# Copies of x's rows by tokens: pinned on ScalarE and placed later, with the evacuation of the first down columns

## The chip, the cores and the metric

The kernel runs on one core of one Trainium2 chip. The metric is the device time of one execution in microseconds. The page of the profile shows one profiled execution; its own time and the median of three runs stand below.

## The reference

Two layers of a decoder trunk on 256 tokens of width 1024, in float32, then a final norm:

```python
def rmsnorm(x, g):
    y = x32 * lax.rsqrt(jnp.mean(x32 * x32, axis=-1, keepdims=True) + EPS)
    return y.astype(x.dtype) * g

def swiglu(x, w_gate, w_up, w_down):
    return (jax.nn.silu(x @ w_gate) * (x @ w_up)) @ w_down
...
    for l in range(DEPTH):
        x = x + 0.5 * swiglu(rmsnorm(x, ffn1_norm[l]), ffn1_w_gate[l], ffn1_w_up[l], ffn1_w_down[l])
...
        x = x + odd_mixer(h, od_w_in[i], od_w_out[i], rel_bias)
        x = x + memory_cross_attention(rmsnorm(x, xa_norm[l]), mem_n, xa_w_q[l], xa_w_kv[l], xa_w_o[l])
        x = x + 0.5 * swiglu(rmsnorm(x, ffn2_norm[l]), ffn2_w_gate[l], ffn2_w_up[l], ffn2_w_down[l])
    return rmsnorm(x, final_norm)
```

The hidden width of each SwiGLU is 2816, that is 22 tiles of 128. The change lies in the last one (ffn2 of layer 1) and the final norm.

## The kernel before

**Products.** x is held by channels: 128 channels on the partitions, 8 tiles, 256 tokens along the row. A float32 product is made of three TensorE passes with fp32r operands: each operand is split into a high part and a low part, and high x high, high x low and low x high are added in PSUM. So each weight tile goes through two steps: ScalarE copies it to `whi` (line 143), VectorE makes `wlo = raw - whi` (line 144). The class `Stream` runs this: SyncE loads chunks of 16 weight tiles (1 MB, line 117) into four `raw` buffers, and blocks of 8 tiles are split into five pairs of `whi` and `wlo`. A block's split can start when TensorE is done with the block five before; a raw buffer is loaded again when VectorE has read it.

**The last SwiGLU.** Its hidden rows are computed with tokens on the partitions, in groups of four tiles (`rows_of`, lines 575 to 577). Each group is turned back to hidden-by-token form by `turned_back`: VectorE transposes 32 x 32 squares (line 545), GpSimd's queue writes them to a DRAM tile `turn` and reads them back in four pieces (lines 547 and 549), and ScalarE and VectorE split the result into `h` (lines 557 and 558). The last such group has two tiles, 20 and 21; its target buffer is named `v`, so its read is `v<-turn` and its split is `h<-v`.

**The last down product** (`down_tok`) has tokens on the partitions, so that its result is already in the output's order. It multiplies `h` by the down weights (lines 791 to 793). First come columns 0 to 511 for both halves of the tokens (two PSUM tiles named `acc`), over all 22 hidden tiles, two at a time. Then come columns 512 to 1023, in three regions: tokens 0 to 127 whole (a PSUM tile named `sc`), tokens 128 to 255 in two halves of 256 columns (`acc`). The first 14 hidden tiles run for all three regions together, the last 8, whose splits stay in four buffers, run region by region.

**The residual by tokens.** For the final sum x is needed with tokens on the partitions. `to_tokens` writes x to a DRAM tile `tok`; `from_tokens` reads it into a tile named `bias` in four pieces on GpSimd's queue (line 839); `natural` copies it into `y`, a tile in the slot named `k2` (shown as `k`), in 16 ScalarE copies of 128 x 128 (line 847). `evac_tok` then adds half the down product (line 804), sums the squares (line 807), multiplies by the final norm's factors (GpSimd, line 810, or VectorE, line 814), and for the last columns scales by the norm and stores (lines 817 to 821).

**What sets the order.** `Order` keeps a model clock in nanoseconds. `pe.after(delay, fn, cost)` puts a task on a heap at the model time plus the delay; the fillers (matmul parts) move the clock by their cost. A task's place in the program comes from this. Behind it a scheduler may move instructions on an engine, except those passed through `tc.keep_in_program_order`, which stay in the written order. The splits of `h` in `turned_back` are pinned in this way; the copies at line 847 are not. Every engine runs its instructions in order, so an instruction that waits for a semaphore holds all behind it.

Of the kernel before, what the change touches and what calls it, by code (L numbers as in the profile page):

```python
# [17 lines left out]
AF = mybir.ActivationFunctionType  # L18
# [5 lines left out]
P = 128  # L24
# [216 lines left out]
def paired(t):  # L241

    return t.rearrange("p (b a) -> p a b", b=2)
# [22 lines left out]
def build(nc, tc, ctx, a):  # L266
# [18 lines left out]
    def w2():  # L285
        return act.tile([P, 512], F32, name="w2", bufs=6)
# [28 lines left out]
    pe = Order()  # L315
# [192 lines left out]
    def to_tokens(tok, k):  # L508


        t = act.tile([P, 2 * S], F32, name="q2", bufs=2)
        tc.keep_in_program_order(nc.vector.transpose(t.rearrange("q (a g j) -> q g a j", a=4, g=4),
                                                     x[:, k:k + 2].rearrange("p k (u a i) -> p (k u) a i", u=2, a=4)))
        tc.keep_in_program_order(nc.sync.dma_start(tok[k // 2], t))
# [19 lines left out]
    def ffn(which, layer, n, nxt, first=False, last=False):  # L534
# [206 lines left out]
        def have(ks):  # L741
            return lambda: math.inf if any(h[k] is None for k in ks) else 0.0
# [26 lines left out]
        def down_tok():  # L769

            late = 2 * (ws.BUFS - 1)
            pss, got, mean = {}, {}, [EPS, EPS]

            def part(fs, *regions):

                c = regions[0][1] // 512

                def go():  # L780
                    for f in fs:
                        if (f, c) not in got:
                            got[f, c] = ws.take(f"{which}_w_down", layer, f * P, c * 512, 4)
                        for reg in regions:
                            u, c0, c1 = reg
                            if f == 0:
                                pss[reg] = (sc_tile if c == 1 and c1 - c0 == 512 else acc_tile)()[:, :c1 - c0]
                            ps = pss[reg]
                            wh, wl = (paired(w)[:, (c0 - c * 512) // 2:(c1 - c * 512) // 2] for w in got[f, c])
                            hh, hl = (h[f].v[:, u, m] for m in range(2))  # L790
                            nc.tensor.matmul(ps, hh, wh, start=f == 0, stop=False)  # L791
                            nc.tensor.matmul(ps, hh, wl, start=False, stop=False)  # L792
                            nc.tensor.matmul(ps, hl, wh, start=False, stop=f == FT - 1)  # L793
                    if fs[-1] == FT - 1:
                        for u, c0, c1 in regions:
                            pe.after(0 if c else 6000, lambda u=u, at=slice(c0, c1), ps=pss[u, c0, c1]: evac_tok(u, at, ps), 0)

                return have(fs), go, sum(len(fs) * (c1 - c0) * 654 // 512 for _, c0, c1 in regions)

            def evac_tok(u, at, ps):  # L800
                xtok = back["y"]
                y = xtok[:, u, at]
                g = gfin[at.start // 512][:, at.start % 512:at.start % 512 + at.stop - at.start]
                nc.vector.scalar_tensor_tensor(y, ps, 0.5, y, op0=ALU.mult, op1=ALU.add)  # L804
                ms = act.tile([P, 1], F32, name="mean", bufs=4)
                junk = w2()[:, :at.stop - at.start]
                nc.vector.tensor_tensor_reduce(junk, y, y, 1.0 / D, mean[u], ALU.mult, ALU.add, ms)  # L807
                mean[u] = ms
                if at.stop < D:
                    nc.gpsimd.tensor_tensor(y, y, g, op=ALU.mult)  # L810
                    return
                r = act.tile([P, 1], F32, name="rcol", bufs=2)
                nc.gpsimd.tensor_tensor(r, ms, mhalf[:, 0:1], op=ALU.pow)
                nc.vector.tensor_tensor(y, y, g, op=ALU.mult)
                out = a["out"][u * P:(u + 1) * P]
                cuts = (0, 384, 704, D)
                nc.scalar.activation(xtok[:, u, :cuts[1]], xtok[:, u, :cuts[1]], AF.Copy, scale=r)
                nc.scalar.dma_start(out[:, :cuts[1]], xtok[:, u, :cuts[1]])
                for i, j in zip(cuts[1:], cuts[2:]):
                    nc.vector.tensor_scalar(xtok[:, u, i:j], xtok[:, u, i:j], r, None, op0=ALU.mult)  # L820
                    nc.sync.dma_start(out[:, i:j], xtok[:, u, i:j])

            end = range(FT - late, FT)
            right = ((0, 512, D), (1, 512, 768), (1, 768, D))
            return [part(range(i, i + 2), (0, 0, 512), (1, 0, 512)) for i in range(0, FT, 2)] + [
                part(range(FT - late), *right)] + [part(end, reg) for reg in right]
# [5 lines left out]
        if last:  # L832
            gfin = []
            tok, back = dram.tile([KT // 2, P, 2 * S], F32, name="tok"), {}

            def from_tokens():
                t = act.tile([P, 2 * D], F32, name="bias", bufs=1)
                for b in range(4):
                    tc.keep_in_program_order(nc.gpsimd.dma_start(
                        t[32 * b:32 * b + 32].rearrange("i (g z) -> i g z", g=16),  # L840
                        tok.rearrange("k (p i) (a z) -> a i (k p) z", p=4, a=4)[b]))
                v = t.rearrange("q (k p m u j) -> q u k m p j", k=4, p=4, m=2, u=2)

                def natural(k):
                    y = back["y"] = back.get("y") or act.tile([P, 2, D], F32, name="k2", bufs=1)
                    for u in range(2):
                        nc.scalar.activation(y[:, u, k * P:(k + 1) * P].rearrange("q (p j) -> q p j", p=4),  # L847
                                             v[:, u, k // 2, k % 2], AF.Copy)

                for k in range(KT):  # L850
                    pe.after(15000+700*k, lambda k=k: natural(k), 0)

            def last_factors():
                gfin.extend(act.tile([P, 512], F32, name="p2", bufs=4) for _ in range(2))
                src = a["final_norm"]
                for i, g in enumerate(gfin):
                    nc.sync.dma_start(g, bass.AP(tensor=src.tensor, offset=src.offset + i * 512, ap=[[0, P], [1, 512]]))

            pe.after(90000, last_factors, 0)
            for k in range(0, KT, 2):  # L860
                pe.after(16000 + 9000 * (k // 2), lambda k=k: to_tokens(tok, k), 0)
            pe.after(114500, from_tokens, 0)
        at = AT.get((which, layer))
        groups = [f0 for f0 in range(0, FT, 4) if at is None or f0 != SEVEN]
# [602 lines left out]
```

## Time and profile before

| | |
|---|---|
| three runs | 967.06, 958.13, 960.61 us (median 960.61) |
| the profiled execution | 960.96 us, span 958.9 us |
| TensorE busy | 947.4 us (99%), 5796 matmuls |
| VectorE, ScalarE, GpSimd busy | 726.1 (76%), 596.6 (62%), 119.2 us (12%) |
| HBM read and written | 220.81 MB and 16.80 MB, 248 GB/s over the span |
| last matmul | starts at 951.45 us |

A row of a timeline has the start, the duration, the engine, the line of the kernel, the operation, the tiles (out<-in without buffer numbers) and the count; in brackets stands how long the engine was idle before it, and what released it. Times count from the span's start. TensorE's rows are matmuls (PE) and weight loads (PEld); since matmuls are pipelined, their rate is read from the distance between starts and not from the duration. A row of the windows has, for a stretch, the busy time of PE, PEld, VectorE (DVE), ScalarE (ACT) and GpSimd (POOL), then the granted TensorE clock as a share of full speed, the share of the DMA engines and GB/s.

### The profile page before, as it was taken

Reading aid. Unit: us, or ns where it says so; the run is one execution under the profiler, and the core shown is the slowest. Engines: PE = TensorE matmul, PEld = TensorE weight load, DVE = VectorE, ACT = ScalarE, POOL = GpSimd, SP = SyncE. Lnnn points to the kernel's source line nnn. Section 1 sums busy time; section 2 is a strip of 40 time slices with the busy share of each in tenths; the row PEclk is TensorE's granted clock in tenths of the full one; section 3 lists DMA queues with packets and bytes.
Section 4 is the critical chain, followed back from the end, with each engine's and each line's share of the span. In section 5 each row is a group of like instructions: output and inputs, shape, how many; then the busy total and the mean of one; then the engine's idle time right before and its main releaser. Section 6 shows DMA issues by size and latency. Waiting matters only on the chain. (4 is left out here: it accounts for less than half of the span.)

```text
span 958.9 us, 15176 instructions
## 1 busy us (share of the span) xinstructions
PE 947.4 (99%) x5796; PEld 868.9 (91%) x5796; DVE 726.1 (76%) x1153; ACT 596.6 (62%) x984; POOL 119.2 (12%) x207
## 2 busy tenths in 40 slices
PE   9999999999999999999999999999999999999987
PEld 8888899999999888889988888999999998888876
DVE  7667667788878886976778697677777789688563
ACT  7555555697658866555576565556775787565451
POOL 0412210001000111121001112100000010202311
PEclk9999999999999999999999999999999999999999
DMA  9999975555536899889759978855534479999841
GB/s 375 314 349 327 327 230 211 180 188 198 183 133 247 233 262 335 254 303 335 246 176 268 334 235 300 288 204 194 218 133 176 150 246 304 274 321 316 260 148 44
DMA packets 39368, 235.44 MB, mean 246 GB/s; under 512 B 5624, under 2 KB 6648, under 8 KB 14720
## 3 DMA queue, kind: packets, MB, share of 16 engines
q1 hardware_dynamic: 26928, 182.43, 52.2%
q0 software_dynamic: 11792, 51.42, 20.7%
q8 instruction: 45, 0.74, 0.3%
q10 hardware_dynamic: 576, 0.64, 0.2%
q14 instruction: 27, 0.22, 0.1%
HBM read 220.81 MB, written 16.80 MB: 248 GB/s over the span
## 5 line engine op out<-in xcount | busy, mean ns | idle before, releaser
L144 DVE TENSOR_TENSOR wlo<-raw,whi 128x1024 fp32r<-128x1024 f32 (+2 forms) x363 | 409.2, 1139 | 145.7 <-ACT whi L143 143.1
L143 ACT ACTIVATE whi<-raw 128x1024 fp32r<-128x1024 f32 (+2 forms) x363 | 353.3, 985 | 235.7 <-PE acc L577 81.0
L576 PE MATMUL acc<-wlo,x 128*128 128x512 f32 x528 | 200.6, 380 | 0.0
L577 PE MATMUL acc<-whi,x 128*128 128x512 f32 x528 | 200.1, 380 | 0.0
L575 PE MATMUL acc<-whi,x 128*128 128x512 f32 x528 | 195.9, 381 | 0.0
L576 PEld LDWEIGHTS acc<-wlo,x 128*128 128x128 f32 x528 | 100.0, 189 | 14.7 <-DVE wlo L144 0.7
L577 PEld LDWEIGHTS acc<-whi,x 128*128 128x128 f32 x528 | 100.1, 189 | 14.0
L575 PEld LDWEIGHTS acc<-whi,x 128*128 128x128 f32 x528 | 99.9, 189 | 14.1
L418 PE MATMUL acc<-h,whi 128*128 128x512 f32 x330 | 108.5, 382 | 0.0
L419 PE MATMUL acc<-h,wlo 128*128 128x256 f32 x330 | 89.9, 273 | 0.0
L425 PE MATMUL acc<-h,wlo 128*128 128x256 f32 x322 | 87.7, 275 | 0.0
L424 PE MATMUL acc<-h,whi 128*128 128x256 f32 x322 | 87.7, 275 | 0.0
L423 PE MATMUL acc<-h,whi 128*128 128x256 f32 x322 | 86.5, 277 | 0.0
L425 PE MATMUL acc<-x,wlo 128*128 128x256 f32 x304 | 84.1, 278 | 0.0
L424 PE MATMUL acc<-x,whi 128*128 128x256 f32 x304 | 83.8, 277 | 0.0
L423 PE MATMUL acc<-x,whi 128*128 128x256 f32 x304 | 83.3, 278 | 0.0
L418 PEld LDWEIGHTS acc<-h,whi 128*128 128x128 f32 x330 | 62.4, 189 | 8.6
L419 PEld LDWEIGHTS acc<-h,wlo 128*128 128x128 f32 x330 | 63.3, 192 | 0.2
L424 PEld LDWEIGHTS acc<-h,whi 128*128 128x128 f32 x322 | 61.7, 192 | 0.1
L425 PEld LDWEIGHTS acc<-h,wlo 128*128 128x128 f32 x322 | 61.7, 192 | 0.1
L423 PEld LDWEIGHTS acc<-h,whi 128*128 128x128 f32 x322 | 60.6, 192 | 0.4 <-DVE x L486 0.2
L424 PEld LDWEIGHTS acc<-x,whi 128*128 128x128 f32 x304 | 58.2, 192 | 0.2
(274 smaller groups left out, 1735.4 us busy)
## 6 DMA issues: line engine op xcount, KB each, us to landing
raw<-in_w SPq DMA_DIRECT2D x165, 1024.0 KB, 6.8
bias<-in_w POOLq DMA_DIRECT2D x12, 1024.0 KB, 12.5
k<-in_w POOLq DMA_DIRECT2D x9, 1024.0 KB, 9.4
turn<-v POOLq DMA_DIRECT2D x9, 512.0 KB, 3.3
v<-turn POOLq DMA_DIRECT2D x36, 128.0 KB, 6.7
dists<-line POOLq DMA_DIRECT2D x2, 1536.0 KB, 12.6
raw<-in_memT SPq DMA_DIRECT2D x3, 1024.0 KB, 4.8
turn<-kT POOLq DMA_DIRECT2D x6, 512.0 KB, 9.2
```

Of the source, the lines that this page charges most:

```text
L143: for ins in (self.nc.scalar.activation(hi[:, at], src, AF.Copy), self.nc.vector.tensor_tensor(lo[:, at], src, hi[:, at].bitcast(F32), op= ...
L144: self.nc.vector.tensor_tensor(lo[:, at], src, hi[:, at].bitcast(F32), op=ALU.subtract)):
L418: nc.tensor.matmul(ps, w[0], x2.both, start=start, stop=False)
L419: nc.tensor.matmul(ps[:, :S], w[1], x2.high, start=False, stop=stop)
L423: nc.tensor.matmul(ps[:, :S], w[0], x2.high, start=start, stop=False)
L424: nc.tensor.matmul(ps[:, :S], w[0], x2.low, start=False, stop=False)
L425: nc.tensor.matmul(ps[:, :S], w[1], x2.high, start=False, stop=stop)
L575: nc.tensor.matmul(ps[u], xh, wh, start=k == 0, stop=False)
L576: nc.tensor.matmul(ps[u], xh, wl, start=False, stop=False)
L577: nc.tensor.matmul(ps[u], xl, wh, start=False, stop=k == KT - 1)
```

## The change

The 16 copies of x's rows by tokens are passed through `tc.keep_in_program_order`, so that they stay where they are written, and their delay behind `from_tokens` goes from 15000 + 700 k to 28000 + 700 k ns of the model clock. The evacuation of columns 0 to 511 of the down product gets a delay of 15000 ns where it had 6000.

```diff
                     if fs[-1] == FT - 1:
                         for u, c0, c1 in regions:
-                            pe.after(0 if c else 6000, lambda u=u, at=slice(c0, c1), ps=pss[u, c0, c1]: evac_tok(u, at, ps), 0)
+                            pe.after(0 if c else 15000, lambda u=u, at=slice(c0, c1), ps=pss[u, c0, c1]: evac_tok(u, at, ps), 0)
...
                 def natural(k):
                     y = back["y"] = back.get("y") or act.tile([P, 2, D], F32, name="k2", bufs=1)
                     for u in range(2):
-                        nc.scalar.activation(y[:, u, k * P:(k + 1) * P].rearrange("q (p j) -> q p j", p=4),
-                                             v[:, u, k // 2, k % 2], AF.Copy)
+                        tc.keep_in_program_order(nc.scalar.activation(
+                            y[:, u, k * P:(k + 1) * P].rearrange("q (p j) -> q p j", p=4), v[:, u, k // 2, k % 2], AF.Copy))
 
                 for k in range(KT):
-                    pe.after(15000+700*k, lambda k=k: natural(k), 0)
+                    pe.after(28000+700*k, lambda k=k: natural(k), 0)
```

On ScalarE, in the last down product, the order before is as follows. `whi<-raw` is the split of a block of weights, `k<-bias` a copy of x's rows, `h<-v` the split of hidden tiles 20 and 21.

```order
L557 ACTIVATE h<-kT 128x2x128 x4
L143 ACTIVATE whi<-raw 128x1024 x5
L847 ACTIVATE k_9791<-bias 128x128 x14
L557 ACTIVATE h<-v 128x2x128 x2
L847 ACTIVATE k_9791<-bias 128x128 x2
L143 ACTIVATE whi<-raw 128x1024 x11
```

At the same place ScalarE's order is now:

```order
L557 ACTIVATE h<-kT 128x2x128 x4
L143 ACTIVATE whi<-raw 128x1024 x3
L557 ACTIVATE h<-v 128x2x128 x2
L143 ACTIVATE whi<-raw 128x1024 x9
L847 ACTIVATE k_10026<-bias 128x128 x16
L143 ACTIVATE whi<-raw 128x1024 x4
```

The 16 copies stood after the fifth split behind `h<-kT`, 14 of them ahead of `h<-v`; now they stand after the twelfth, and `h<-v` stands after the third.

On VectorE, the same stretch before; `wlo<-raw,whi` is the low part of a weight block, L804 the evacuation of columns 0 to 511, and L807 its sum of squares.

```order
L558 TENSOR_TENSOR h<-kT,h 128x2x128 x4
L144 TENSOR_TENSOR wlo<-raw,whi 128x1024 x5
L558 TENSOR_TENSOR h<-v,h 128x2x128 x2
L144 TENSOR_TENSOR wlo<-raw,whi 128x1024 x4
L804 SCALAR_TENSOR_TENSOR k_9791<-acc,k_9791 128x512 x2
```

VectorE's order there now:

```order
L558 TENSOR_TENSOR h<-kT,h 128x2x128 x4
L144 TENSOR_TENSOR wlo<-raw,whi 128x1024 x3
L558 TENSOR_TENSOR h<-v,h 128x2x128 x2
L144 TENSOR_TENSOR wlo<-raw,whi 128x1024 x9
L804 SCALAR_TENSOR_TENSOR k_10026<-acc,k_10026 128x512 x2
```

The evacuation moved from behind the ninth low part after `h<-kT` to behind the twelfth; four low parts follow it where there were seven. It depends on the copies, since both write `y`. The orders of TensorE, GpSimd and SyncE stay as they were.

## The prediction

> **What bounds the kernel now.** I read the page's head first, then every wait of TensorE, then the end of the program engine by engine, since the order moves instructions there alone.
>
> Head of the page, and all waits of TensorE's matmuls (line waited for: us in total, times, longest):
>
> ```profile
> span 958.9 us, 15176 instructions
> PE 947.4 (99%) x5796; PEld 868.9 (91%) x5796; DVE 726.1 (76%) x1153; ACT 596.6 (62%) x984; POOL 119.2 (12%) x207
> PE acc L791 <- ACT h L557: 3.5, 1, 3.5
> PE tr L313 <- PEq L1420: 0.8, 1, 0.8
> ```
>
> TensorE sets the time: 947.4 of 958.9 us. It waits once inside the program, for ScalarE's split of h at L557. The timeline of TensorE there (start, duration, what):
>
> ```profile
> 912.01 0.38 PE L791 MATMUL acc<-whi,h 128*128 128x512 f32 x1
> ...
> 914.17 0.38 PE L792 MATMUL acc<-wlo,h 128*128 128x512 f32 x1
> 914.38 0.38 PE L793 MATMUL acc<-whi,h 128*128 128x512 f32 x1
> 918.26 0.79 PE L791 MATMUL acc<-whi,h 128*128 128x512 f32 x1 [3.50 <-ACT h L557]
> ...
> 921.41 0.47 PE L792 MATMUL acc<-wlo,h 128*128 128x512 f32 x1
> 921.71 0.38 PE L793 MATMUL acc<-whi,h 128*128 128x512 f32 x1
> ```
>
> Matmuls of this shape start 0.216 us apart: the 11 steps from 912.01 to 914.38 make 0.2155 each. The next was due at 914.60 and came at 918.26. The eight from 918.26 to 921.41 are slower; the ninth starts at 921.71, back at full pace. Two stretches of the windows show why (PEclk, the granted clock, is third from the end):
>
> ```profile
> 918.00:920.00 2.00, 1.74 (x4) 1.46 (x5) 0.87 (x3) 2.00 (x6) 0.00 (x0) 0.54 0.00 0
> 920.00:922.00 2.00, 2.00 (x7) 1.57 (x7) 2.00 (x2) 2.00 (x3) 0.00 (x0) 0.60 0.00 0
> ```
>
> So after its pause TensorE was granted about half its clock for 3.45 us. ScalarE's timeline says who was late:
>
> ```profile
> 901.48 4.83 ACT L143 ACTIVATE whi<-raw 128x1024 fp32r<-128x1024 f32 x5
> 915.00 2.90 ACT L847 ACTIVATE k<-bias 128x128 f32<-128x128 f32 x14 [8.69 <-DMA bias<-tok]
> 917.81 0.70 ACT L557 ACTIVATE h<-v 128x256 fp32r<-128x256 f32 x2
> 918.42 0.49 ACT L847 ACTIVATE k<-bias 128x128 f32<-128x128 f32 x2
> 918.82 5.02 ACT L143 ACTIVATE whi<-raw 128x1024 fp32r<-128x1024 f32 x5
> 925.41 1.06 ACT L143 ACTIVATE whi<-raw 128x1024 fp32r<-128x1024 f32 x1 [1.57 <-PE acc L793]
> 928.05 1.06 ACT L143 ACTIVATE whi<-raw 128x1024 fp32r<-128x1024 f32 x1 [1.57 <-PE acc L793]
> ```
>
> The copies of x's rows (L847) stand ahead of the h split and wait 8.69 us for their own transfer. The split is what TensorE needs; the copies are not. The transfers, on GpSimd's queue: the issues with their times, the time from issue to landing of v<-turn (the split's source) and then of bias<-tok (min/median/max), and the chain's row for the last piece of bias<-tok.
>
> ```profile
> 901.05 2.18 POOL L549 DMA_DIRECT2D v<-turn  x4 [5.68 <-ACT h L557]
> 903.23 2.59 POOL L839 DMA_DIRECT2D bias<-tok  x4
> DMA to landing us min/median/max: 2.2/2.2/2.3
> DMA to landing us min/median/max: 3.5/5.8/9.7
> 905.16 9.73 DMA bias<-tok
> ```
>
> The split's data landed by 901.05 + 2.18 + 2.3 = 905.5 at the latest, nine microseconds before TensorE needed it; the copies' data landed at 914.89.
>
> **The change, part by part.** All sums run against the profiled execution, 960.96 us around a span of 958.9, so 2.06 us lie outside the span. It stands 0.35 us above the median of the three runs shown, 960.61.
>
> *The copies leave the front of the split: the gain.* On ScalarE the two h splits now follow three weight splits, and the 16 copies come nine weight splits later. If TensorE does not pause, the matmul that started at 921.71 starts at 914.60 + 8 x 0.2155 = 916.32. That is 5.39 us: 3.66 us of pause (918.26 less 914.60) and 1.73 us of slow clock. All of it lies on the path, since TensorE shows no other wait from there to its last matmul.
>
> *What is late next on ScalarE.* The three weight splits at 4.83 / 5 = 0.97 each end at 904.4. The h pair then waits until at most 905.5 and takes 0.70, to 906.2. The fourth weight split ends at 907.2 (1.06 after). TensorE needs it at 912.01, 12 x 0.2155 before 914.60, and VectorE's low half of it 0.2 us later. VectorE's side:
>
> ```profile
> 902.55 5.77 DVE L144 TENSOR_TENSOR wlo<-raw,whi 128x1024 fp32r<-128x1024 f32 x5 [0.44 <-ACT whi L143]
> 918.24 0.76 DVE L558 TENSOR_TENSOR h<-v,h 128x256 fp32r<-128x256 f32 x2 [9.92 <-ACT h L557]
> 924.44 1.28 DVE L804 SCALAR_TENSOR_TENSOR k<-acc,k 128x512 f32<-128x512 f32 x2
> ...
> 926.86 0.08 DVE L807 DVE_READ_ACCUMULATOR2_ANT mean<- 128x1 f32 x1
> 926.86 6.78 DVE L144 TENSOR_TENSOR wlo<-raw,whi 128x1024 fp32r<-128x1024 f32 x4
> ```
>
> Low halves take 5.77 / 5 = 1.15 us. Three end at 906.0, the h pair at about 907.0 (0.76), the fourth low half at 908.4: 3.8 us before 912.2. No cost.
>
> *The copies in their new place.* TensorE starts on the right columns at 914.60 + 12 x 0.2155 = 917.19, and uses a block of weights each 2.64 us (928.05 less 925.41, ScalarE pacing itself by TensorE). Five buffers hold splits, so the seventh block's split can start when TensorE is done with the second, at 917.19 + 2 x 2.64 = 922.47, and ends at 923.4. There the 16 copies start; their data, at 914.89, is 8.5 us early. They take 2.90 + 0.49 = 3.39 us, to 926.8. The eighth block's split, possible from 925.1, starts 1.7 us late and ends at 927.9; TensorE needs it at 917.19 + 7 x 2.64 = 935.7. ScalarE catches up at the ninth. No cost.
>
> *The first evacuation follows the copies.* VectorE's two L804 and two L807 with their accumulator reads, 924.44 to 926.94 = 2.50 us, now wait for the copies and run from 926.8 to 929.3, with the eighth block's low half queued behind. That half takes between 1.15 and 6.78 / 4 = 1.70 us, the second while GpSimd multiplies beside it, and ends at 931.0. The slack to 935.7 is 4.7 us. If all this cover were gone (the copies exposed, 3.39, and the evacuation, 2.50), it would cost 5.9 us. GpSimd's two multiplications then run to about 933, long before the last columns:
>
> ```profile
> 926.47 3.83 POOL L810 TENSOR_TENSOR k<-k,p 128x512 f32<-128x512 f32 x2 [20.65 <-ACT whi L143]
> ```
>
> [...] The trace shows four low halves in 6.78 us beside both multiplications, 1.70 each against 1.15 alone. [...]
>
> *The queues.* GpSimd's and SyncE's own orders do not change. The weight loads do move in time: each waits for VectorE to free a raw buffer.
>
> ```profile
> 904.94 2.60 SPq L117 DMA_DIRECT2D raw<-in_w  x2
> 921.14 2.60 SPq L117 DMA_DIRECT2D raw<-in_w  x2
> DMA to landing us min/median/max: 4.8/6.7/10.1
> ```
>
> The load that left at 921.14 now leaves at about 910.7, as soon as the low half of the block after the h pair's is done, and shares the queues with bias<-tok. The longest landing, 10.1 us, gives 920.8; its split is due on ScalarE at 926.8. If bias<-tok doubles its 9.73 us, it lands at 924.6, 1.2 us after the copies could start, inside the slack. No cost.
>
> *The end.* The last matmul starts at 951.45 and the span ends at 958.9; these 7.4 us of evacuation and stores are the same instructions in the same order, and move along.
>
> Bounds of the gain: nothing, if another wait takes the pause's whole place; 5.39 us, if none does. I take 5.39, because each candidate above has at least 3.8 us of slack. Sum: 960.96 - 5.39 = **955.6 us** (span 953.5), 0.5% under the median before.
>
> **The rivals.**
>
> *The pause moves to the split's own transfer.* The fourth weight split is now queued behind the h pair, which waits for v<-turn. If v<-turn lands at L, the chain is h 0.70, weight split 1.06, low half 1.15: TensorE waits if L + 2.9 passes 912.2, so from L = 909.3. For: transfers beside it took up to 9.73 us. Against: these four took 2.2 to 2.3, and start before bias<-tok. At 9.73 after the last issue, about 902.7, L is 912.4 and the pause 3.1; with the same slow clock behind it, 1.73, the gain shrinks to 0.6: 960.4. A pause alone would give 958.7. [...] Chance 0.08.
>
> *The stall is this execution's own.* Had bias<-tok landed 4 us sooner, the old order would hardly have paused. If the timed executions do not have the pause, the change removes nothing: 960.6. Against: even the fastest of them, 958.13, is 2.5 us above my 955.6, room for a pause. Chance 0.09.
>
> *Slower: the copies hold the last weights.* Copies, evacuation and the eighth block form one chain on two engines. If bias<-tok, now beside one more load, lands later than 923.4 + 4.7 = 928.1, TensorE pauses before its eighth block; from about 932 the pause and its slow clock outweigh the 5.39 gained. Landing at 936 costs 7.9 + 1.7 - 5.4 = 4.2 us more: 965.2. Against: that needs a transfer of 31 us where 9.73 was the longest of the four. Chance 0.04.
>
> *More than the sum.* The pause is as long as the transfer is late, so it differs between executions: the run of 967.06 lies 6.1 us above the profiled one. If such pauses are typical, the kernel after is still at 955.6 but the gain passes 1%. If the 2.83 us by which 958.13 undercuts the profiled execution came from elsewhere in the program, the time can fall to 952.8. Chance 0.09 for both together.
>
> **How the numbers follow.** My forecast, the pause gone, has 0.70. A measurement of this kernel tells about 1% (9.6 us) from no change, and 5.39 us is below that. The range runs from 952.8 (the fastest run's margin) to 960.6 (no gain), and holds all but the slower rival and the odd disturbed run. Faster by over 1%: 0.08, from the last case. Slower by over 1%: 0.03, most of the slower rival. Within 1%: 0.89.
>
> **What would show it.** TensorE's waits keep only the 0.8 us at the start; PEclk stays at 1.00 from 914 to 946; the L557 pair on h from v runs near 905; L847 is one group of 16 from about 923.4, without a wait for bias<-tok; the first L804 comes near 926.8; the last matmul starts near 946.1. A TensorE wait on L143 or L144 near 912 would show the first rival, near 935 the slower one. A span still near 959 without such a wait would prove the sum wrong.

## The result, and the profile after

| | before | after |
|---|---|---|
| median | 963.36 us (14 runs) | 955.68 us (14 runs) |
| lowest and highest | 958.13, 968.45 | 955.0, 958.39 |
| the profiled execution | 960.96 | 955.00 |

The ratio is 0.9923, with a 95% interval of 0.9902 to 0.9944: a gain of 0.8%, clear of no change, though the prediction held that a measurement here could tell only about 1%. The time forecast, 955.6 us, is within 0.1 us of the median after. The gain is larger than forecast, 7.7 us between the medians against 5.39, because the median before rose from 960.61 (three runs) to 963.36 (fourteen).

The head of the page after, and all that TensorE's matmuls wait for in it:

```profile
span 953.1 us, 15179 instructions
PE 945.1 (99%) x5796; PEld 867.1 (91%) x5796; DVE 725.6 (76%) x1153; ACT 596.4 (63%) x984; POOL 118.7 (12%) x207
PE tr L313 <- PEq L1420: 0.8, 1, 0.8
```

The wait of 3.5 us for the h split is gone, and nothing took its place. The windows where the clock had been 0.54 and 0.60:

```profile
918.00:920.00 2.00, 2.00 (x15) 1.87 (x14) 1.23 (x1) 0.43 (x2) 0.00 (x0) 1.00 0.99 414
920.00:922.00 2.00, 2.00 (x16) 1.89 (x16) 1.23 (x1) 0.66 (x1) 0.00 (x0) 1.00 1.04 434
```

TensorE's timeline has the last matmul before the old pause and the last of the program:

```profile
913.96 0.38 PE L793 MATMUL acc<-whi,h 128*128 128x512 f32 x1
914.18 0.38 PE L791 MATMUL acc<-whi,h 128*128 128x512 f32 x1
...
945.64 0.28 PE L793 MATMUL acc<-whi,h 128*128 128x256 f32 x1
```

From the one to the other it took 951.45 - 914.38 = 37.07 us before and takes 945.64 - 913.96 = 31.68 now: 5.39 less, as summed. Of the 5.96 us between the two profiled executions 0.42 us was already gained before 913.96, outside the change, and 0.15 lies outside the span. ScalarE's timeline after:

```profile
900.50 2.94 ACT L143 ACTIVATE whi<-raw 128x1024 fp32r<-128x1024 f32 x3
908.59 0.72 ACT L557 ACTIVATE h<-v 128x256 fp32r<-128x256 f32 x2 [5.14 <-DMA v<-turn]
909.22 4.83 ACT L143 ACTIVATE whi<-raw 128x1024 fp32r<-128x1024 f32 x5
...
923.20 3.29 ACT L847 ACTIVATE k<-bias 128x128 f32<-128x128 f32 x16
926.40 2.17 ACT L143 ACTIVATE whi<-raw 128x1024 fp32r<-128x1024 f32 x2
```

The copies run as one group from 923.20 without a wait, as forecast (923.4). The h pair, however, waited 5.14 us for its own transfer and ran at 908.59 instead of 905.5. GpSimd's issues, and the landing of v<-turn and of bias<-tok (min/median/max), say why:

```profile
902.11 2.17 POOL L549 DMA_DIRECT2D v<-turn  x4 [4.27 <-ACT whi L143]
904.28 2.58 POOL L839 DMA_DIRECT2D bias<-tok  x4
DMA to landing us min/median/max: 4.7/4.9/5.2
DMA to landing us min/median/max: 9.0/9.7/10.5
```

v<-turn left 1.06 us later than before and took 5.2 us, not 2.3. VectorE's timeline shows what this left:

```profile
909.04 0.76 DVE L558 TENSOR_TENSOR h<-v,h 128x256 fp32r<-128x256 f32 x2 [3.96 <-ACT h L557]
910.29 6.90 DVE L144 TENSOR_TENSOR wlo<-raw,whi 128x1024 fp32r<-128x1024 f32 x6 [0.49 <-ACT whi L143]
...
924.73 1.29 DVE L804 SCALAR_TENSOR_TENSOR k<-acc,k 128x512 f32<-128x512 f32 x2 [0.17 <-ACT k L847]
...
927.47 5.35 DVE L144 TENSOR_TENSOR wlo<-raw,whi 128x1024 fp32r<-128x1024 f32 x3 [0.23 <-ACT whi L143]
```

The first of the six low parts ended at 910.29 + 6.90 / 6 = 911.44. TensorE needed it one matmul after 914.18 - 12 x 0.2155 = 911.59, at 911.81. Of the 3.8 us of slack in the prediction, 0.4 was left in this execution. It is not always so: in three more profiles of this order on the engines (e1, e8 and e10 below) v<-turn took at most 2.4 us, and the h pair ran at 903.6 to 904.6 without waiting for it.

### The profile page after: what moved, and what is told of

Read it like the earlier page. It is cut to its first block, busy times and chain, and to the rows that moved or that the text cites. A ratio compares the mean times of both kernels' runs of the same rounds, so it can differ in the third digit from the quotient of the medians.

```text
span 953.1 us, 15179 instructions
## 1 busy us (share of the span) xinstructions
PE 945.1 (99%) x5796; PEld 867.1 (91%) x5796; DVE 725.6 (76%) x1153; ACT 596.4 (63%) x984; POOL 118.7 (12%) x207
## 4 chain that ended last, share of the span: by engine, by line
PE 99%; DMA 0%; DVE 0%; POOLq 0%; issue 0%; DVEq 0%
PE acc L576 12%; PE acc L577 12%; PE acc L575 12%; PE acc L418 8%; PE acc L423 7%; PE acc L424 7%; PE acc L425 7%; PE acc L419 4%; PE sc L418 3%; PE tr L685 2%; PE tr L684 2%; PE tr L686 2%; PE sc L575 2%; PE sc L576 2%; PE sc L577 2%; PE acc L793 2%
```

## The experiments

**What makes the pause: the wait or the place?** In e3 the copies lose their pin, with all delays of the change kept. The scheduler puts them behind five weight splits after `h<-kT`, not twelve.

```diff
-                        tc.keep_in_program_order(nc.scalar.activation(
-                            y[:, u, k * P:(k + 1) * P].rearrange("q (p j) -> q p j", p=4), v[:, u, k // 2, k % 2], AF.Copy))
+                        nc.scalar.activation(y[:, u, k * P:(k + 1) * P].rearrange("q (p j) -> q p j", p=4),
+                                             v[:, u, k // 2, k % 2], AF.Copy)
```

> The changed kernel with the pin taken off the copies: the scheduler puts them behind five weight splits instead of twelve, behind the h pair, where they still wait for bias<-tok. Theory (what counts is whether anything that TensorE needs stands behind the copies' wait): the h pair is free, but the first weights of the right columns now wait; bias<-tok lands near 915, copies end near 918.3, weight split and low part near 920.4 against a need at 917.4, so a pause of about 3 us and 958.5, or 960 with a slow clock behind it. Rival (only the h pair behind the copies mattered): 955.6.

Measured: 961.57 us (median of 10, 955.17 to 964.81), ratio 0.9996, interval 0.9965 to 1.0026: the gain is gone. TensorE's waits and ScalarE's timeline of e3, then its windows:

```profile
PE sc L791 <- ACT whi L143: 3.1, 1, 3.1
PE sc L792 <- DVE wlo L144: 0.8, 1, 0.8
PE acc L792 <- DVE wlo L144: 0.5, 1, 0.5
909.50 0.72 ACT L557 ACTIVATE h<-v 128x256 fp32r<-128x256 f32 x2 [5.34 <-DMA v<-turn]
916.52 3.31 ACT L847 ACTIVATE k<-bias 128x128 f32<-128x128 f32 x16 [4.39 <-DMA bias<-tok]
```

```profile
920.00:922.00 2.00, 0.48 (x1) 0.19 (x1) 1.19 (x2) 2.00 (x3) 0.00 (x0) 1.00 0.00 0
922.00:924.00 2.00, 1.91 (x8) 1.80 (x9) 2.00 (x3) 2.00 (x3) 0.00 (x0) 0.62 0.49 102
924.00:926.00 2.00, 2.00 (x9) 1.73 (x8) 2.00 (x4) 0.57 (x1) 0.00 (x0) 0.52 0.96 401
```

The pause is now in front of the first weights of the right columns (`sc`), which stand behind the copies. What must not stand behind this transfer is anything that TensorE needs soon, not the h pair alone. The size was too small in the expectation: the transfer came 1.5 us later than assumed, and a slow clock followed (0.62 and 0.52). From the last matmul ahead of those of tiles 20 and 21 (914.74) to the last of the program (952.51) it takes 37.77 us, 6.1 more than 31.68. The wait of 0.5 us comes earlier, at 912.48, and is the prediction's first rival in its own place: the fourth weight split stands behind the h pair, as in the changed kernel, and the pair waited 5.34 us for v<-turn.

In e4 the kernel before keeps its delays; its copies are pinned and read x as it lies by channels, so that they wait for no transfer. bias<-tok still runs. Three weight splits, not five, now stand ahead of the h pair.

```diff
-                        nc.scalar.activation(y[:, u, k * P:(k + 1) * P].rearrange("q (p j) -> q p j", p=4),
-                                             v[:, u, k // 2, k % 2], AF.Copy)
+                        tc.keep_in_program_order(nc.scalar.activation(
+                            y[:, u, k * P:(k + 1) * P].rearrange("q (p j) -> q p j", p=4),
+                            x[:, k, u * P:(u + 1) * P].rearrange("q (p j) -> q p j", p=4), AF.Copy))
```

> The kernel before with its delays, the copies still mostly ahead of the h pair (14 of 16) and pinned, but read from x as it lies by channels, which is in SBUF all along; bias<-tok still runs and nobody reads it. The output is therefore not the sum with x by tokens. Theory (the wait for the transfer is the cost, not the copies' 3.4 us): no pause, 955.6. Rival (the copies' own time in front of the h pair costs): a pause of up to 3.4 us, 957 to 959.

Measured: 956.03 us (median of 10, 954.92 to 957.22), ratio 0.9935, interval 0.9913 to 0.9958. ScalarE's timeline, with 14 copies still ahead of the h pair:

```profile
905.67 1.70 ACT L847 ACTIVATE k<-x 128x128 f32<-128x128 f32 x8
...
909.02 0.71 ACT L557 ACTIVATE h<-v 128x256 fp32r<-128x256 f32 x2
```

TensorE did not wait for the h pair: the copies' own 3 us in front of it cost nothing. The profiled execution, 956.81 us, has one wait of 0.8 us near 905, on a low part ahead of these copies; it is of the kind met in e2 below. The wait for the transfer is the cost, and with it goes the wide spread of the kernel before.

**Does the pause follow the transfer?** In e6 and e7 bias<-tok is transferred twice over, in the kernel before and in the changed one.

```diff
-                for b in range(4):
+                for b in (0, 1, 2, 3) * 2:
                     tc.keep_in_program_order(nc.gpsimd.dma_start(
```

> The kernel before, with bias<-tok transferred twice over (same source, same target, 2 MB instead of 1), so that it lands about 10 us later. Theory (the pause lasts as long as the transfer is late): landing near 925, copies to 928, h pair to 928.4 against a need at 914.6, so a pause of about 13.5 us and 970 to 973. Rival (the pause is not set by this transfer): 960 to 964 as before.

> The changed kernel, with bias<-tok transferred twice over. Its copies could start at 923.3; a landing near 925 delays copies, first evacuation and the eighth weight block by about 2 us, inside the prediction's slack of 4.7 us. Theory: 955.5 to 957, no wait of TensorE near 935. Rival (the late copies hold the last weights, the slower case of the prediction): a pause near 935 and 958 or more.

Measured: e6 970.5 us (median of 10), ratio 1.0072, interval 1.0048 to 1.0097. e7 955.87 us (median of 5, 955.44 to 955.94), ratio 0.9918, interval 0.9890 to 0.9947. TensorE's wait and ScalarE's copies in e6, then ScalarE's copies in e7:

```profile
PE acc L791 <- ACT h L557: 7.0, 1, 7.0
922.06 2.90 ACT L847 ACTIVATE k<-bias 128x128 f32<-128x128 f32 x14 [10.91 <-DMA bias<-tok]
```

```profile
926.13 3.31 ACT L847 ACTIVATE k<-bias 128x128 f32<-128x128 f32 x16 [2.63 <-DMA bias<-tok]
```

The profiled execution of e6, 965.4 us, was its quickest; its transfer landed at 922.0 and not near 925, and its pause was 7.0 us, about half the 13.5 expected. The median is where the theory put it. In e7 the copies waited 2.63 us in their new place, and TensorE waited for nothing. So the slack ahead of the last weights holds at least this much; the slower rival did not come even with the transfer doubled.

**Is the spread of the kernel before the same pause?** The kernel before was profiled three more times, unchanged.

> The kernel before, profiled a second time, to see whether its spread of 955.4 to 968.5 is the pause. Theory: its time above 955.5 equals the pause of TensorE in front of the matmul that needs hidden tiles 20 and 21, plus the slow clock behind it, and the pause equals the lateness of bias<-tok. For a time T: pause plus slow clock within 1 us of T less 955.5. Rival: a pause near 3.6 us whatever T, the rest elsewhere.

> The kernel before, profiled a third time; so far both its profiles lay near 961, below the middle of its timed executions. Theory: with T its time, pause plus slow clock is T less 955.4, within 1 us. Rival: a pause of 3.5 us whatever T.

> The kernel before, profiled a fourth time, for the same reading: theory, pause plus slow clock is T less 955.4 within 1 us; rival, a pause of 3.5 us whatever T.

"Stretch" is the time from the start of the last matmul before the pause to the start of the program's last; 31.68 us is its length without a pause.

| profile of before | time | from, to | stretch | less 31.68 | time less that |
|---|---|---|---|---|---|
| first | 960.96 | 914.38, 951.45 | 37.07 | 5.39 | 955.57 |
| e5 | 960.61 | 914.35, 951.34 | 36.99 | 5.31 | 955.30 |
| e11 | 962.51 | 914.06, 952.97 | 38.91 | 7.23 | 955.28 |
| e12 | 967.15 | 916.23, 957.86 | 41.63 | 9.95 | 957.20 |

In e12 another 1.0 us is an earlier pause on a weight block's low part (below), and 0.9 the sum of six shorter gaps beside it; less these, it stands at 955.3 like the others. The rows of e12: TensorE's waits, the chain's last piece of the transfer, and the copies.

```profile
PE acc L791 <- ACT h L557: 7.8, 1, 7.8
PE acc L792 <- DVE wlo L144: 0.8, 1, 0.8
909.03 11.96 DMA bias<-tok
921.10 2.90 ACT L847 ACTIVATE k<-bias 128x128 f32<-128x128 f32 x14 [12.42 <-DMA bias<-tok]
```

The transfer landed at 921.0 here, against 914.9 in the first profile: issued 3.9 us later and 2.2 us longer under way. The theory, a loss within 1 us of the time less 955.5 (e5) or 955.4, held in e5 and e11. In e12 it missed: 11.75 us were expected and 9.95 found, and the earlier pause and gaps make up the difference. The rival of a fixed 3.5 us fell. What makes GpSimd's queue run late in one execution and not in another was not tried.

**The two delays apart.** In e8 the evacuation's delay is put back. Delaying the evacuation alone, or pinning the copies alone, leaves the order of every engine in the program as it was before, so neither was run.

```diff
-                            pe.after(0 if c else 15000, lambda u=u, at=slice(c0, c1), ps=pss[u, c0, c1]: evac_tok(u, at, ps), 0)
+                            pe.after(0 if c else 6000, lambda u=u, at=slice(c0, c1), ps=pss[u, c0, c1]: evac_tok(u, at, ps), 0)
```

> The changed kernel with the evacuation's delay put back to 6000 ns; copies pinned and at 28000 ns. The order on the engines is that of the changed kernel, since the evacuation depends on the copies. Theory (the move of the copies does all): 955.7, as the changed kernel. Rival (the evacuation's delay has a share): above 957.

Measured: 955.53 us (median of 6, 955.3 to 956.49), ratio 0.9916, interval 0.9889 to 0.9944. The evacuation follows the copies by its dependence; its own delay does nothing.

**What is left: the changed kernel's own spread.** e1 and e10 are the changed kernel again, each beside another version on the same chip. In e2 the split of hidden tiles 20 and 21 is emitted later; in e9 those of tiles 16 to 19 too, so that one more weight split stands ahead of each.

```diff
-            pe.after((34000 if f0 < 8 else 28000 if f0 < SEVEN else 22000) if sevens else
+            pe.after((34000 if f0 < 8 else 28000 if f0 < SEVEN else 25000 if last and f0 == FT - 2 else 22000) if sevens else
```

```diff
-            pe.after((34000 if f0 < 8 else 28000 if f0 < SEVEN else 22000) if sevens else
+            pe.after((34000 if f0 < 8 else 28000 if f0 < SEVEN else 27000 if last and f0 >= FT - 6 else 22000) if sevens else
```

> The changed kernel as it stands, beside the others of this group. Theory (before, the pause of TensorE lasts as long as bias<-tok is late, so it differs from execution to execution; the changed order does not wait for it): 955 to 956.5 with a narrow spread, the kernel before 958 to 968 with a wide one. Rival (the wide spread of before comes from elsewhere in the program): the changed kernel would spread by about 10 us too.

> The changed kernel, with the split of hidden tiles 20 and 21 emitted 3000 ns later on the model clock, so that on ScalarE and VectorE one more weight split (tiles 18 and 19) stands ahead of it. In the trace of the changed kernel the h pair waited 5.14 us for v<-turn, and the weight split behind it was ready only about 0.4 us before TensorE needed it. Theory (the executions of the changed kernel at 957 to 958.4 are those in which v<-turn lands a little later and TensorE pauses): 955.2, none above 956.5. Rival (these executions are late for another reason): the same spread as the changed kernel, 955.0 to 958.4.

> The changed kernel with the splits of hidden tiles 16 to 19 (h<-kT) and 20, 21 (h<-v) both emitted 5000 ns later on the model clock: on ScalarE and VectorE one more weight split stands ahead of each. The traces of the two runs before that kept a pause (0.8 us on L792, waiting for a low part, near 904) show it behind the h<-kT splits, which wait for kT<-turn. Theory (the rest of the changed kernel's spread is this wait): 955.2 to 955.4, none above 956.5. Rival (the rest comes from elsewhere): the changed kernel's 955.0 to 958.4.

> The changed kernel once more, beside the one with both splits later on the same chip. Theory: 955.7 with executions to 958, 0.3 to 0.5 us above its neighbour. Rival: no difference from its neighbour in middle or spread.

| | median | lowest to highest | ratio, interval |
|---|---|---|---|
| e1, changed kernel | 955.97 (12 runs) | 955.15 to 964.6 | 0.9935, 0.9908 to 0.9963 |
| e2, split of 20 and 21 later | 955.65 (12) | 955.07 to 959.64 | 0.9936, 0.9915 to 0.9957 |
| e10, changed kernel | 955.84 (9) | 954.96 to 961.9 | 0.9942, 0.9912 to 0.9972 |
| e9, splits of 16 to 21 later | 955.19 (6) | 954.94 to 955.34 | 0.9922, 0.9898 to 0.9946 |

e1 missed its expectation of a narrow spread: four of its twelve executions lie above 956.5, and the one at 964.6 makes its range 9.5 us, against 12.5 for the 35 of the kernel before beside it. e2 missed its expectation: three of its executions lie above 956.5. Its profile shows another pause, on the low part of a weight block, and ScalarE's timeline has the splits of tiles 16 to 19 waiting ahead of that block's split:

```profile
PE acc L792 <- DVE wlo L144: 0.8, 1, 0.8
901.51 1.34 ACT L557 ACTIVATE h<-kT 128x256 fp32r<-128x256 f32 x4 [6.36 <-DMA kT<-turn]
902.75 3.89 ACT L143 ACTIVATE whi<-raw 128x1024 fp32r<-128x1024 f32 x4
```

The same wait row stands in e4 and e12. It is the mechanism of this change a second time: a split that waits for a transfer, with weights behind it. e9 moves both out of the way, and its profile, like its expectation, has no wait but the start's:

```profile
PE tr L313 <- PEq L1420: 0.8, 1, 0.8
906.30 0.72 ACT L557 ACTIVATE h<-v 128x256 fp32r<-128x256 f32 x2 [3.39 <-DMA v<-turn]
```

Its six executions lie within 0.4 us, its neighbour's nine within 6.9. The median is 0.65 us lower, a little more than expected; the two ratios' intervals overlap, so a gain over the changed kernel is likely but not shown. The two single executions at 964.6 and 961.9 of the changed kernel were not profiled, and their cause stays open.

## Why the prediction was right

**The sum.** 960.96 less 5.39 gave 955.6; measured were 955.00 in the profile and 955.68 as the median. The term itself, pause plus slow clock, was removed to the hundredth (37.07 against 31.68).

**The gain was mis-sized where it rested on one execution.** The forecast of 0.5% took the pause of the one profiled execution as typical. Three more profiles cost 5.31, 7.23 and 9.95 us by the same reckoning. The prediction had this as a case of its own, the pause as long as the transfer is late, at a chance of 0.09 shared with another case; it is what happened, though the gain, 0.8%, stayed within 1%. The time after came out all the same, because the profiled execution less its own pause is the same 955.3 to 955.6 whichever of the first three profiles one starts from.

**ScalarE's next wait.** "No cost" was right, the slack of 3.8 us was not. It rested on v<-turn landing within 2.3 us; with 5.2 us and a later issue 0.4 us was left. The first rival's mechanism is real: e3 shows it at the h pair, 0.5 us, and e2, e4 and e12 at the split one group earlier, 0.8 us each.

**The copies and the evacuation.** The copies started at 923.20 (forecast 923.4) and took 3.29 us (3.39). The evacuation began at 924.73, not 926.8: VectorE waited only for the copies that it reads, not for all 16, which took until 926.49 (the seventh ended at about 923.20 + 7 x 3.29 / 16 = 924.6). Beside GpSimd's multiplications three low parts took 5.35 us, 1.78 each (forecast up to 1.70). GpSimd's row for both multiplications, then the answers for the first multiplication, the first low part, and the second and third together (count, min/median/max in ns, first and last start):

```profile
926.77 3.83 POOL L810 TENSOR_TENSOR k<-k,p 128x512 f32<-128x512 f32 x2 [19.91 <-ACT k L847]
L810 POOL TENSOR_TENSOR k<-k,p x1: 1612/1612/1612, 926.8 to 926.8; 128x512 f32<-128x512 f32 x1
L144 DVE TENSOR_TENSOR wlo<-raw,whi x1: 1989/1989/1989, 927.5 to 927.5; 128x1024 fp32r<-128x1024 f32 x1
L144 DVE TENSOR_TENSOR wlo<-raw,whi x2: 1210/1756/2301, 929.4 to 931.6; 128x1024 fp32r<-128x1024 f32 x2
```

The eighth block's low part is the first: 1.99 us, longer than forecast, but at its end by 929.46 because the evacuation was early. The first multiplication ended at 926.77 + 1.61 = 928.38, the second at 926.77 + 3.83 = 930.60. The first low part ended 1.1 us after the one, the second (929.4 + 2.30 = 931.7) 1.1 us after the other, and the third, alone, took 1.21. In the first profile of the kernel before it is 1.1 us both times, too: there the two beside the multiplications took 2.30 us each and ended at 929.16 and 931.4, the multiplications at 928.08 and 930.30, and the two low parts behind them took 1.21 each. So in both profiles each of the two made hardly any headway until the multiplication under way at its start was done, as far as GpSimd's spans, which are rough, can tell: in the profile after, that one still had 0.9 and 1.2 us to run.

**The rival of the stall that is this execution's own** fell: all four profiles of before have it. Not every execution need have it: the quickest timed ones of the kernel before, 955.41 (beside e1) and 955.55 (beside e9), leave almost no room for a pause; they were not profiled. **The slower rival** fell with e7.

## What to carry to other kernels

ScalarE ran its instructions in the program's order here: in the first profile of before the h pair, whose data had landed by 905.5, ran at 917.81, behind 14 copies that had waited 8.69 us for bias<-tok. On such an engine, look at what stands behind each instruction that waits for a transfer; if the bottleneck's next operand is among it, the transfer's lateness becomes a pause, whatever its size in the busy times (here 3.39 us of copies and 0.70 of split, and pauses of 3.3 to 7.8 us in the four profiles of before). Move the waiting instruction behind operands with slack, then look at the next such wait: here it was the h pair's own transfer, with 0.4 us left, and the split one group earlier. Where such a wait ends last, one profile gives the pause of one execution; the spread of the timed runs tells how typical it is.

## What the runs showed of the hardware

The clock cost after a pause varies. The windows of e11 in a row, the granted clock third from the end:

```profile
916.00:918.00 2.00, 0.00 (x0) 0.00 (x0) 0.00 (x0) 2.00 (x12) 0.00 (x0) 0.91 0.03 8
918.00:920.00 2.00, 1.55 (x4) 1.29 (x5) 0.76 (x2) 2.00 (x7) 0.00 (x0) 0.50 0.00 0
920.00:922.00 2.00, 2.00 (x6) 1.58 (x5) 1.92 (x2) 2.00 (x4) 0.00 (x0) 0.50 0.00 0
922.00:924.00 2.00, 2.00 (x6) 1.62 (x5) 2.00 (x3) 0.91 (x2) 0.00 (x0) 0.50 0.81 233
924.00:926.00 2.00, 2.00 (x12) 1.80 (x12) 2.00 (x4) 1.03 (x1) 0.00 (x0) 0.88 1.01 406
```

After an idle time of 4.0 us the matmuls ran at half pace (0.426 us from start to start, against 0.2155) from 918.45 to about 924.4, six microseconds, against 3.45 us in the first profile after a nearly equal idle time of 3.5. Of the 7.23 us lost there 3.06 are slow clock, of the first profile's 5.39 only 1.73 (e5 1.82, e12 2.04). What sets the length of the slow stretch was not shown.

In e3 the clock was still whole behind the first pause of 3.1 us (1.00 from 920 to 922) and fell only behind one matmul and another 0.8 us of waiting (0.62 from 922 to 924, 0.52 from 924 to 926). The shortest single pause with a slow clock behind it is e5's, 3.3 us (0.74 from 918 to 920, 0.50 from 920 to 922). So whether a single pause of 3.1 us is followed by a slow clock, as in the prediction's 960.4, or not, as in its 958.7, stays open.

The transfers of one program differ from execution to execution: the four pieces of bias<-tok took at most 9.7, 9.8, 11.4 and 12.0 us in the four profiles of the kernel before, and those of v<-turn at most 5.2, 2.4 and 2.3 us in three profiles of the changed kernel (the first, e1 and e10), with the same bytes.
